# Encoder block on one core: block differences of the late phases on GpSimd, the output weights' differences made at the end of the attention's branch, an idle run of 11 products

## The chip, the cores and the metric

One core of a Trainium2 chip runs the whole kernel. The core has five engines that run side by side, each with its own queue of instructions: TensorE (PE, matrix products into PSUM), VectorE (DVE), ScalarE (ACT), GpSimd (POOL) and SyncE (SP, which issues most of the DMAs). SBUF is the on-chip memory that all of them read and write, DRAM the large memory behind the DMAs. The metric is the device time of one execution in microseconds (us); lower is better. A time is given as the median of several runs.

## The reference

One encoder block works on a stream of 16 learned tokens and 1024 positions, each of width 1024, in float32. Cut to what matters here:

```python
u = rms_norm(h, pre_w)
z = u @ w_in                            # 1024 x 7680; split into ten parts
rq, rk, rv, rg, aq, ak, av, ag, gr, ga = split(z)
o_r = group_norm(bidirectional_retention(rq, rk, rv)) * silu(rg)     # 4 heads
y_r = o_r @ w_rb
o_a = windowed_attention(aq, ak, av, sink) * silu(ag)                # 8 heads, 2 groups
y_a = o_a @ w_ab
mix = sigmoid(gr) * y_r + sigmoid(ga) * y_a
out = h + rms_norm(mix @ w_o, post_w)   # the 16 learned tokens are dropped
```

Four large products come last: the gate columns of `w_in` (rg, ag, gr, ga: 4096 columns), then `w_rb`, `w_ab` and `w_o` (1024 x 1024 each). They are the four late phases of the kernel.

## The kernel before, in words

**Arithmetic.** Every float32 operand of a product is split in a high part, rounded to TensorE's format (a cast, mostly on ACT), and a low part, operand minus high part (a subtraction, `dve_lo`, on DVE). `mm3` (lines 74 to 79) makes each product of three matmuls: high by high (L76), low by high (L77), high by low (L78). A matmul of the late phases has 128x128 weights and 512 columns.

**The stages in order.** The beginning loads the input, computes the norm and the first projections (0 to about 38 us). Before the first real product stands a run of idle products of zeros into a PSUM bank that nobody reads (`idle`, L310 to L313); their operand `xm` is ready very early, while the first real operand needs a load, a scaling and a split. Retention and attention follow, with their projections, until about 545 us. Then come the late phases.

**The late phases** are run by `class Phase` (L955 on): z (the 16 gate units of 256 columns, from about 545 to 797 us), r (`w_rb`, to 874), a (`w_ab`, to 951) and o (`w_out`, to 1036). A unit is a product of a 1024 x 256 left side with a 1024 x 1024 right side, each cut into 2 x 2 blocks, and is made with seven block products in place of eight (Winograd's form). A block product is a *job*: 4 x 3 matmuls. The right side of a phase (the transposed normed input in z, the gated branch output in r and a, `w_out` in o) has seven forms, each with high and low part: the blocks B11, B21, B22 and the differences T1 to T4, all held in SBUF for the whole phase. The left side's forms are made unit by unit: `prepare` (L979) makes a job's sums on DVE and then splits them (`split`, L973: cast on ACT, low part on DVE) into `lh` and `ll`. There are 6 buffers of each, and `run` (L1193) lets `prepare` go 6 jobs ahead of the job that it issues to PE (LEAD = 6). In the profile `lhz` and `llz` are the two parts in phase z; `llr`, `lla`, `llo` those of the other phases. The tile `bz`, `br`, `ba`, `bo` is the PSUM bank of a job.

**The hand-over from phase to phase.** Near the end of a phase, when a form of the old right side has been read for the last time, its place is filled with the same form of the next phase's. `refill(nm, src)` (L1143) gives a table from a job's number, counted back from the phase's end (-16 to -1), to what is done behind that job. Through z and r:

- loads of the four blocks of the new right side, each as four pieces 128x512 (256 KB) in buffers of `stage` (tags sg0 with 7 and sg1 with 8 buffers);
- `plain(...)`: `split_b` of a piece (L950; cast on ACT, low part on DVE) into its place among the forms;
- `minus(...)` (L1154, its instruction at L1155): one block difference of a piece, 128x512, on DVE. T1 = B12 - B11, T2 = B22 - B11, T3 = B22 - B12, T4 = B21 - B11, up to the names of the buffers, so 4 differences for each of the four T's, 16 at a hand-over. Each is written over one of its sources, and split after that.

At the third hand-over, a to o, the table is another one (`if nm == "a"`): only B11, B21 and B22 are loaded and split. The four differences of `w_out` were made long before, in phase z. There, behind the jobs 12k + 16 for k = 0 to 3, `pre_load` (L764) loads four pieces of `w_out`; behind the jobs 12k + 22 `pre_split` (L771) makes of them four differences on DVE (L776), four casts on ACT (L778), four low parts on DVE, and stores each of the eight results to DRAM (`pre_d`, L69). A list `near` holds the latest addition that a phase made out of PSUM on DVE, and a difference is ordered behind that one (`issue_after`). At the hand-over `get_pre` (L1128) loads the finished parts into their places, 8 loads of 1 MB or 768 KB and 2 of 256 KB.

**Other work in the late phases.** `combine` (L1052 on) adds the products of a unit out of PSUM on DVE and copies some on ACT; `z_post` scales and gates the results and stores them, `y_post` (L1275) multiplies by the gates, and in phase a adds to the stored sum `mx_d` by four accumulating DMAs that POOL issues (L1289); `o_post` makes the norm, the residual and the output.

**What sets the order.** Each engine takes its instructions strictly in the order of its queue; it waits, with all that is behind, where an operand is not there. The order within a queue is set when the kernel is built, by a planner that works from the order of the Python calls, its own cost model of the engines, and `issue_after`. DMAs of one queue are issued in the order of that queue too: nearly all loads and stores of the late phases are on SP's, those at L1289 on POOL's.

Of the kernel before, what the change touches and what calls it, by code (L numbers as in the profile page):

```python
# [7 lines left out]
F32 = mybir.dt.float32  # L8
R = mybir.dt.float32r
AF = mybir.ActivationFunctionType  # L10
ALU = mybir.AluOpType
# [5 lines left out]
P = 128  # L17
# [22 lines left out]
def block_kernel(ctx: ExitStack, tc: tile.TileContext, x0, xT, x, meta, w_in, w_rb, w_ab, w_out, post_w,  # L40
                 rope, tab, out):
    nc = tc.nc
# [12 lines left out]
    def bank(tag, name):  # L55
# [10 lines left out]

    e_d = {(u, p): dram.tile([P, 512], F32, tag=f"e{u}{p}", name=f"e{u}_{p}") for u in PRE for p in PRE[u]}
    xs_d = [dram.tile([4, P, 2, 512], F32, tag=f"xs{i}", name=f"xs{i}") for i in range(2)]
    pre_d = {n: [dram.tile([P, 4, 512], F32, tag=f"pre{n}{s}", name=f"pre{n}{s}") for s in range(2)]  # L69
             for n in ("T1", "T2", "T3", "T4")}  # L70

    latest = []

# [17 lines left out]
    def dve_lo(o, i, hi):  # L91
        return nc.vector.tensor_tensor(o, i, hi.bitcast(F32), ALU.subtract).ins  # L92
# [173 lines left out]
    with tc.tile_pool(name="setup", bufs=1, reuse_waits="tile") as st:  # L266
# [42 lines left out]

        idle = pj("idle")  # L310
        zeros = xm.rearrange("p k e -> p (k e)")
        for i in range(8):
            nc.tensor.matmul(idle[:, 0:KT * (32 + NM)], zeros[:, 0:P], zeros, start=True, stop=True)  # L313


# [12 lines left out]
        for k in range(KT):  # L328
            t = xr[k]
# [431 lines left out]

    xsum = {}

    def pre_load(k, src):  # L764

        w[k] = {}
        for i, j in ((0, 0), (0, 1), (1, 1), (1, 0)):
            w[k][i, j] = t = stage(f"w{i}{j}{k}", 1)
            src(t, 4 * i + k, j)

    def pre_split(k, behind):  # L771

        x = w.pop(k)
        for n, o, a, b in SUMS:
            with tc.issue_after(behind):
                nc.vector.tensor_tensor(x[o], x[a], x[b], ALU.subtract)  # L776
            h, l = (stage(f"w{n}{k}{e_}", s, R) for s, e_ in enumerate("hl"))
            nc.scalar.copy(h, x[o])  # L778
            nc.sync.dma_start(pre_d[n][0][:, k], h.bitcast(F32))
            dve_lo(l, x[o], h)  # L780
            nc.sync.dma_start(pre_d[n][1][:, k], l.bitcast(F32))

    w, near = {}, []
    gates = [U_G + u for u in range(4)] + [U_AG + u for u in range(4)] + [U_GR + u for u in range(8)]

    def pre_fetch(u):
# [149 lines left out]
    def right(n, s, k):  # L936
        if n == "T4" and k == 3:
            return margins[s], lambda t: t.rearrange("p (a c) -> p a c", a=KT)
        return B[n][s][:, k], lambda t: t
# [4 lines left out]
    def stage(name, j=0, dt=F32):  # L944
        return (yp if j else lp).tile([P, 512], dt, tag=f"sg{int(j)}", bufs=8 if j else 7, name=name)
# [179 lines left out]
            return l[:14] + o[:5] + l[14:15] + o[5:] + l[15:]  # L1125
        return [(u + e_, p) for u in range(0, n, 2) for p in (ORDER if u else first) for e_ in range(2)]

    def get_pre(n):  # L1128
        for s in range(2):
            m = B[n][s].shape[1]  # L1130
            nc.sync.dma_start(B[n][s].bitcast(F32), pre_d[n][s][:, 0:m])
            if m < 4:
                d, as_ = right(n, s, m)
                nc.sync.dma_start(d.bitcast(F32), as_(pre_d[n][s][:, m]))

    def get_sum(n):
        for k in range(4):
            t = stage(f"x{n}{k}", n in ("T2", "T3"))
# [4 lines left out]
    def refill(nm, src):  # L1143

        x = {}

        def load(i, j):
            def f():
                for k in range(4):
                    x[i, j, k] = t = stage(f"{nm}{i}{j}{k}", j)  # L1150
                    src(t, 4 * i + k, j)
            return f

        def minus(o, a, b):  # L1154
            nc.vector.tensor_tensor(x[*o], x[*a], x[*b], sub)  # L1155

        def plain(n, i, j):
            def f():
                for k in range(4):
                    split_b(n, k, x[i, j, k])  # L1160
            return f

        def t1():
            for k in range(4):
                minus((0, 0, k), (0, 1, k), (0, 0, k))
                split_b("T1", k, x[0, 0, k])

        def t2():
            for k in range(4):
                minus((0, 0, k), (1, 1, k), (0, 0, k))  # L1170
                split_b("T2", k, x[0, 0, k])

        def t3():
            for k in range(4):
                minus((0, 1, k), (1, 1, k), (0, 1, k))

        def b21():
            for k in range(4):
                split_b("B21", k, x[1, 0, k])
                minus((0, 0, k), (1, 0, k), (0, 0, k))  # L1180

        def got(n):
            return lambda: get_pre(n)

        if nm == "a":
            return {-16: [load(0, 0)], -14: [load(1, 1)], -13: [plain("B11", 0, 0)], -11: [got("T1")],
                    -10: [load(1, 0)], -9: [got("T2")], -7: [plain("B21", 1, 0)], -5: [got("T3")],
                    -3: [plain("B22", 1, 1)], -1: [got("T4")]}
        return {-16: [load(0, 0), load(0, 1)], -14: [load(1, 1)], -13: [plain("B11", 0, 0)], -11: [t1],
                -10: [load(1, 0)], -9: [t2, t3], -7: [b21], -5: [plain("T3", 0, 1)], -3: [plain("B22", 1, 1)],  # L1190
                -1: [plain("T4", 0, 0)]}

    def run(phases):  # L1193
# [7 lines left out]

        for u in (0, 1):
            hooks.setdefault(len(jobs) - len(ph_o.seq) - 11 + u, []).insert(0, lambda u=u: ph_o.block(u, "A11"))
        for k in range(4):
            hooks[12 * k + 16] = [lambda k=k: pre_load(k, act_src(w_out))]
            hooks[12 * k + 22] = [lambda k=k: pre_split(k, near[0])]
        n = 0
        for i, (ph, u, p) in enumerate(jobs):
            while n < min(i + LEAD, len(jobs)):
# [475 lines left out]
```

## Time and profile before

Three runs of the kernel took 1042.65, 1043.71 and 1046.04 us. The profiled execution took 1044.06 us; its trace spans 1042.3 us from the first to the last instruction.

| what | value |
|---|---|
| median of the runs | 1043.71 us |
| profiled execution | 1044.06 us |
| span of its trace | 1042.3 us |
| mean granted TensorE clock | 0.998 of full speed |
| instructions | 17315, of which 5880 matmuls |

The page of the profile has, in its second part, the span in 40 equal slices of 26 us, each digit the busy share of that slice in tenths:

```profile
## 2 busy tenths in 40 slices
PE   8999999999999999999999999999999999999997
PEld 8998999989989888988888888777888788788886
DVE  7786769758876778778769988998899899778665
ACT  5541332523423466664676554555557446334443
POOL 3345244243342433444310000000000000111032
PEclk9999999999999999999999999999999999999999
```

The late phases are the slices from the 21st on. In them DVE is at 8 or 9 tenths up to the 34th, the hand-over from r to a, and POOL does next to nothing from the 23rd to the 34th. Slices are means: a wait of one microsecond does not show in them.

A list of waits has a line for each engine and tile: who waited, for what, how many us in total, how often, and the longest. A table of stretches gives the busy time of each engine in one stretch of time. A timeline gives the start and the duration of every instruction. Busy times of PE are partly modelled, since matmuls overlap in its pipeline; the number of matmuls that start in a stretch is the safer reading.

### The profile page before, as it was taken

The page shows a single profiled execution, that of the slowest core. Times are in us where ns is not written, and L with a number is a line of the kernel's source. Part 1 is how long each engine was busy: PE and PEld are TensorE (multiplying, and loading weights), DVE is VectorE, ACT ScalarE, POOL GpSimd, SP SyncE. Part 2 cuts the span into 40 slices and gives each one's busy share as a digit, 9 for nine tenths or more (in the row PEclk, how much of TensorE's full clock was granted, in tenths as well). Part 3 has the DMA queues.
Part 4 walks back from the last instruction along what each step waited for, and adds up shares of the span by engine and source line. Part 5 has one row for each costly group of instructions (what it writes and reads, how often), then busy time and mean ns, then how long its engine had stood idle before and what let it go on. Part 6 is the DMA issues. An engine that isn't in the chain of part 4 may idle for free. (4 is left out here: it accounts for less than half of the span.)

```text
span 1042.3 us, 17315 instructions
## 1 busy us (share of the span) xinstructions
PE 1025.3 (98%) x5880; PEld 898.8 (86%) x5880; DVE 834.9 (80%) x1802; ACT 502.5 (48%) x1129; POOL 227.9 (22%) x368
## 2 busy tenths in 40 slices
PE   8999999999999999999999999999999999999997
PEld 8998999989989888988888888777888788788886
DVE  7786769758876778778769988998899899778665
ACT  5541332523423466664676554555557446334443
POOL 3345244243342433444310000000000000111032
PEclk9999999999999999999999999999999999999999
DMA  9434123243241467675558679899925746789464
GB/s 355 164 84 90 62 45 89 76 79 112 80 93 62 102 174 188 179 194 157 171 174 322 216 255 311 309 317 346 392 106 178 251 156 222 234 219 336 130 122 81
DMA packets 98841, 188.45 MB, mean 181 GB/s; under 512 B 13025, under 2 KB 37633, under 8 KB 98193
## 3 DMA queue, kind: packets, MB, share of 16 engines
q1 hardware_dynamic: 81200, 162.89, 46.4%
q0 software_dynamic: 10176, 14.73, 9.5%
q10 hardware_dynamic: 7376, 9.73, 2.7%
q8 instruction: 46, 0.75, 0.3%
q14 instruction: 43, 0.34, 0.1%
HBM read 124.32 MB, written 57.68 MB: 175 GB/s over the span
## 5 line engine op out<-in xcount | busy, mean ns | idle before, releaser
L1289 POOL DMA_DIRECT2D mx_d<-c1a x4 | 3.6, 890 | 398.1 <-DVE c1a L1280 398.1
L77 PE MATMUL bz<-big,llz 128*128 128x512 f32 x192 | 74.8, 390 | 0.3 <-DVE llz L92 0.3
L76 PE MATMUL bz<-big,lhz 128*128 128x512 f32 x192 | 74.0, 390 | 1.1 <-ACT lhz L976 1.1
L78 PE MATMUL bz<-big,lhz 128*128 128x512 f32 x192 | 74.2, 389 | 0.0
L76 PE MATMUL pv<-wh,big 128*128 128x256 f32 x256 | 72.8, 284 | 0.0
L77 PE MATMUL pv<-wh,big 128*128 128x256 f32 x256 | 72.7, 284 | 0.0
L78 PE MATMUL pv<-wl,big 128*128 128x256 f32 x256 | 72.7, 284 | 0.0
L76 PE MATMUL bz<-T,lhz 128*128 128x512 f32 x176 | 68.2, 390 | 1.4 <-DVE u2z L1066 1.3
L77 PE MATMUL bz<-T,llz 128*128 128x512 f32 x176 | 68.6, 390 | 0.9 <-DVE llz L92 0.9
L78 PE MATMUL bz<-T,lhz 128*128 128x512 f32 x176 | 68.5, 389 | 0.0
L76 PE MATMUL paq<-big,wh 128*128 128x512 f32 x128 | 51.5, 403 | 0.0
L1429 ACT ACTIVATE p<-raw,nm 128x337 f32<-128x337 f32 (+1 forms) x64 | 35.5, 556 | 33.1 <-DVE nm L1426 31.6
L77 PE MATMUL paq<-big,wl 128*128 128x512 f32 x128 | 50.3, 393 | 0.0
L78 PE MATMUL paq<-big,wh 128*128 128x512 f32 x128 | 50.2, 392 | 0.0
L1442 POOL TENSOR_SCALAR p<-p,den 128x336 f32<-128x336 f32 (+2 forms) x60 | 34.6, 624 | 66.7 <-DVE den L1433 64.1
L76 PEld LDWEIGHTS pv<-wh,big 128*128 128x128 f32 x256 | 48.4, 189 | 0.4
L77 PEld LDWEIGHTS pv<-wh,big 128*128 128x128 f32 x256 | 48.3, 189 | 0.4
L78 PEld LDWEIGHTS pv<-wl,big 128*128 128x128 f32 x256 | 48.2, 188 | 0.3
L76 PEld LDWEIGHTS bz<-big,lhz 128*128 128x128 f32 x192 | 36.0, 188 | 8.8 <-ACT lhz L976 1.5
L92 DVE TENSOR_TENSOR wl<-wr,wh 128x1024 fp32r<-128x1024 f32 x28 | 35.1, 1257 | 10.0 <-POOL wh L89 6.8
L77 PEld LDWEIGHTS bz<-big,llz 128*128 128x128 f32 x192 | 36.0, 188 | 8.1 <-DVE llz L92 0.6
L78 PEld LDWEIGHTS bz<-big,lhz 128*128 128x128 f32 x192 | 36.0, 188 | 7.5
(621 smaller groups left out, 3592.8 us busy)
## 6 DMA issues: line engine op xcount, KB each, us to landing
wrz<-in_w_in_dram SPq DMA_DIRECT2D x32, 512.0 KB, 6.1
wr<-in_w_in_dram SPq DMA_DIRECT2D x29, 512.0 KB, 4.1
we<-in_w_in_dram SPq DMA_DIRECT2D x16, 512.0 KB, 4.3
tg<-tg_d SPq DMA_DIRECT2D x32, 256.0 KB, 4.9
e<-e ACTq DMA_DIRECT2D x20, 256.0 KB, 2.6
e<-e SPq DMA_DIRECT2D x20, 256.0 KB, 4.7
xn<-in_x_dram SPq DMA_DIRECT2D x8, 512.0 KB, 9.0
oTr_d<-ost SPq DMA_DIRECT2D x16, 256.0 KB, 2.1
```

Of the source, the lines that this page charges most:

```text
L76: nc.tensor.matmul(o, ah, bh, start=first, stop=False, **kw)
L77: nc.tensor.matmul(o, al, bh, start=False, stop=False, **kw)
L78: latest[:] = [nc.tensor.matmul(o, ah, bl, start=False, stop=last, **kw).ins]
L92: return nc.vector.tensor_tensor(o, i, hi.bitcast(F32), ALU.subtract).ins
L1289: nc.gpsimd.dma_start(d, to, accum_op=ALU.add)
L1429: last["exp"] = nc.scalar.activation(pp[:, x_, w0 - o:w0 - o + 1 + wid], r[:, 0:1 + wid], AF.Exp, scale=-1.0, bias=nm_[:, x_:x_ + 1], accu ...
L1442: nc.gpsimd.tensor_scalar(v, v, den[:, x_:x_ + 1], 1.0, op0=ALU.mult, op1=ALU.mult)
```

## The change

- The idle run at the beginning has 11 products in place of 8.
- `minus` in `refill` is an instruction of GpSimd (`nc.gpsimd.tensor_tensor`) in place of VectorE.
- `pre_load`, `pre_split`, `get_pre`, the DRAM tiles `pre_d` and the two hooks in phase z that called them are gone. So is the table of its own for the hand-over from a to o: `w_out` is now loaded, subtracted and split at the end of phase a, by the same table as at the other two hand-overs.

```diff
@@ block_kernel @@
-    pre_d = {n: [dram.tile([P, 4, 512], F32, tag=f"pre{n}{s}", name=f"pre{n}{s}") for s in range(2)]
-             for n in ("T1", "T2", "T3", "T4")}
...
-        for i in range(8):
+        for i in range(11):
             nc.tensor.matmul(idle[:, 0:KT * (32 + NM)], zeros[:, 0:P], zeros, start=True, stop=True)
...
-    def pre_load(k, src):
-
-        w[k] = {}
-        for i, j in ((0, 0), (0, 1), (1, 1), (1, 0)):
-            w[k][i, j] = t = stage(f"w{i}{j}{k}", 1)
-            src(t, 4 * i + k, j)
-
-    def pre_split(k, behind):
-
-        x = w.pop(k)
-        for n, o, a, b in SUMS:
-            with tc.issue_after(behind):
-                nc.vector.tensor_tensor(x[o], x[a], x[b], ALU.subtract)
-            h, l = (stage(f"w{n}{k}{e_}", s, R) for s, e_ in enumerate("hl"))
-            nc.scalar.copy(h, x[o])
-            nc.sync.dma_start(pre_d[n][0][:, k], h.bitcast(F32))
-            dve_lo(l, x[o], h)
-            nc.sync.dma_start(pre_d[n][1][:, k], l.bitcast(F32))
-
-    w, near = {}, []
+    near = []
@@ get_pre @@
-    def get_pre(n):
-        for s in range(2):
-            m = B[n][s].shape[1]
-            nc.sync.dma_start(B[n][s].bitcast(F32), pre_d[n][s][:, 0:m])
-            if m < 4:
-                d, as_ = right(n, s, m)
-                nc.sync.dma_start(d.bitcast(F32), as_(pre_d[n][s][:, m]))
-
@@ refill @@
         def minus(o, a, b):
-            nc.vector.tensor_tensor(x[*o], x[*a], x[*b], sub)
+            nc.gpsimd.tensor_tensor(x[*o], x[*a], x[*b], sub)
...
-        def got(n):
-            return lambda: get_pre(n)
-
-        if nm == "a":
-            return {-16: [load(0, 0)], -14: [load(1, 1)], -13: [plain("B11", 0, 0)], -11: [got("T1")],
-                    -10: [load(1, 0)], -9: [got("T2")], -7: [plain("B21", 1, 0)], -5: [got("T3")],
-                    -3: [plain("B22", 1, 1)], -1: [got("T4")]}
         return {-16: [load(0, 0), load(0, 1)], -14: [load(1, 1)], -13: [plain("B11", 0, 0)], -11: [t1],
                 -10: [load(1, 0)], -9: [t2, t3], -7: [b21], -5: [plain("T3", 0, 1)], -3: [plain("B22", 1, 1)],
                 -1: [plain("T4", 0, 0)]}
@@ run @@
-        for k in range(4):
-            hooks[12 * k + 16] = [lambda k=k: pre_load(k, act_src(w_out))]
-            hooks[12 * k + 22] = [lambda k=k: pre_split(k, near[0])]
```

Counted over the whole kernel, DVE has 48 instructions fewer (32 from the gates, 32 differences of the two hand-overs, and 16 low parts more at the third), POOL 48 more, ACT as many as before (16 casts moved from the gates to the third hand-over), SP 54 DMAs fewer (16 loads, 32 stores and 10 loads gone, 4 loads new) and PE three matmuls more.

## The prediction

> **What bounds the kernel now.** I read the page's busy times, then TensorE's list of waits, then busy times in stretches of 20 us, then the timelines.
>
> ```profile
> span 1042.3 us, 17315 instructions
> PE 1025.3 (98%) x5880; PEld 898.8 (86%) x5880; DVE 834.9 (80%) x1802; ACT 502.5 (48%) x1129; POOL 227.9 (22%) x368
> ```
>
> PE (TensorE) is busy 98% of the span, so only the 17.0 us in which it is not, or in which it runs slowly, can be won. The list of waits (engine, line, for whom, us in total, times) has the phases z (gates), r and a (branches):
>
> ```profile
> PE bz L76 <- DVE u2z L1066: 1.3, 1, 1.3
> PE bz L77 <- DVE llz L92: 1.2, 2, 0.9
> PE bz L76 <- ACT lhz L976: 1.1, 1, 1.1
> PE ba L77 <- DVE lla L92: 0.9, 1, 0.9
> PE br L77 <- DVE llr L92: 0.8, 2, 0.6
> ```
>
> Each waits for VectorE (DVE) or for ScalarE's cast beside it. The stretches say where:
>
> ```profile
> 640.00:660.00 20.00, 20.00 (x89) 16.55 (x89) 16.79 (x28) 9.22 (x16) 0.00 (x0) 1.00 0.89 312
> 660.00:680.00 20.00, 18.80 (x82) 15.00 (x81) 18.07 (x31) 8.32 (x15) 0.00 (x0) 1.00 0.97 342
> 680.00:700.00 20.00, 18.69 (x83) 15.18 (x82) 20.00 (x34) 11.93 (x21) 0.00 (x0) 1.00 0.94 296
> 700.00:720.00 20.00, 20.00 (x90) 16.55 (x89) 16.79 (x29) 10.04 (x18) 0.00 (x0) 1.00 1.01 366
> 720.00:740.00 20.00, 19.06 (x85) 15.45 (x84) 17.68 (x30) 10.55 (x19) 0.00 (x0) 1.00 0.98 357
> ...
> 780.00:800.00 20.00, 20.00 (x90) 16.55 (x89) 20.00 (x34) 15.31 (x28) 0.00 (x0) 1.00 0.44 144
> 800.00:820.00 20.00, 19.20 (x84) 15.23 (x83) 19.62 (x33) 10.48 (x19) 0.00 (x0) 1.00 0.85 284
> ...
> 860.00:880.00 20.00, 20.00 (x90) 16.57 (x89) 20.00 (x34) 13.53 (x25) 0.00 (x0) 1.00 0.59 206
> 880.00:900.00 20.00, 19.11 (x83) 15.14 (x82) 19.19 (x32) 9.06 (x16) 0.00 (x0) 1.00 0.82 279
> 900.00:920.00 20.00, 20.00 (x90) 16.58 (x89) 15.29 (x26) 6.09 (x11) 5.24 (x6) 1.00 0.75 184
> 920.00:940.00 20.00, 20.00 (x90) 16.57 (x89) 12.32 (x19) 8.27 (x15) 1.74 (x3) 1.00 0.88 248
> 940.00:960.00 20.00, 20.00 (x90) 16.54 (x89) 17.69 (x31) 9.42 (x16) 1.75 (x2) 1.00 0.96 336
> ```
>
> The columns are PE, weight loads, DVE, ACT and POOL (GpSimd), each in us with its instructions in brackets, then clock, DMA share and GB/s. A full stretch starts 90 products, 0.222 us each. Missing products are lost time: 8 + 7 + 5 = 20 in the gates (4.4 us), 6 where z hands over to r (1.3 us), 7 where r hands over to a (1.6 us). In these stretches DVE is near or at 20 of 20, while POOL has nothing to do from 640 to 900. The hand-over from a to o loses nothing: DVE is idle there for 4.71 + 7.68 + 2.31 = 14.7 us.
>
> The beginning (start, duration, what):
>
> ```profile
> 1.36 2.93 PE L313 MATMUL idle<-xm 128*128 128x384 f32 x8 [1.36 <-DVE warm L207]
> 5.53 0.77 PE L76 MATMUL pq<-big,w 128*128 128x512 f32 x1 [1.24 <-ACT big L333]
> ...
> 7.41 0.63 PE L76 MATMUL pq<-big,w 128*128 128x512 f32 x1
> 7.83 0.63 PE L77 MATMUL pq<-big,w 128*128 128x512 f32 x1
> ...
> 10.65 0.39 PE L76 MATMUL pq<-big,w 128*128 128x512 f32 x1
> 10.88 0.39 PE L77 MATMUL pq<-big,w 128*128 128x512 f32 x1
> ```
>
> A 512-column product starts 0.42 us after the one before until about 10.6 us, and 0.23 us after it from then on: half pace for the first 5.1 us of real work (5.53 to 10.65), after an idle run of 2.93 us and a gap of 1.24 us. The clock column of the stretches does not show this.
>
> **The change, part by part.** Durations are from this one execution, 1044.06 us (span 1042.3), which lies 0.35 us above the median 1043.71 of the runs; I subtract from the execution and then take off 0.35.
>
> ```profile
> L776 DVE TENSOR_TENSOR w<-w,w x16: 679/681/685, 616.8 to 721.0; 128x512 f32<-128x512 f32 x16
> L313 PE MATMUL idle<-xm x8: 522/522/687, 1.4 to 3.8; 128*128 128x384 f32 x8
> L1155 DVE TENSOR_TENSOR z<-z,z 128x512 f32<-128x512 f32 x16 | 10.7, 682 | 0.0
> L195 POOL TENSOR_TENSOR qr<-m_qk,m_qk 128x512 f32<-128x512 f32 x2 | 2.6, 1288 | 4.1 <-DVE m_qk L194 2.7 <-DVE ms L378 1.4
> 780.35 1.89 DVE L1155 TENSOR_TENSOR z<-z,z 128x512 f32<-128x512 f32 x3
> 688.12 0.68 DVE L92 TENSOR_TENSOR wT12l<-w,wT12h 128x512 fp32r<-128x512 f32 x1
> ```
>
> Three in a row take 1.89, so one costs DVE (1.89 - 0.68) / 2 = 0.60 us.
>
> 1. Out of the gates: 16 differences (L776) and 16 low parts (the wT row's kind), 32 x 0.60 = 19.2 us of DVE from 616.8 us to shortly after 721.0 (first and last start of L776); 16 casts on ACT; 16 loads and 32 stores of 256 KB on SP's queue. The lost 20 products lie in that stretch, behind a DVE without a gap. Taking out 4.8 us for each of the four parts leaves DVE some 15 of 20, as in the full stretches. Gain between 0 (if it was the DMA that held the operands) and 4.4; I take 4.4, because the list names DVE and ACT and no DMA.
>
> 2. Idle run 8 to 11: three more at (2.93 - 0.69) / 7 = 0.32 us (0.687, the longest of the eight, for the first to pass through) end at 4.29 + 0.96 = 5.25, before the operand of 5.53. They delay nothing. If full pace follows 5.1 us after an unbroken run begins, as in the rows, and the run now begins at 1.36, it comes at 6.5: slow work falls from 5.1 to 1.0 us, worth (5.1 - 1.0) / 2 = 2.1 us. If the remaining gap of 0.28 still breaks the run, nothing. I take 1.6, nearer to the upper end, since the gap shrinks to a quarter. The order in which PE takes the first pieces changes a little too; no wait stands there, so 0.
>
> 3. Differences of z to r and r to a, 16 each, from DVE to POOL. DVE is freed 16 x 0.60 = 9.6 us at each hand-over; POOL works 16 x 1.29 = 20.6 us in stretches of some 45 us, so it is not the bound by itself. But the engines get in each other's way when both read SBUF:
>
> ```profile
> 54.37 0.41 DVE L92 TENSOR_TENSOR Slf<-Sf,Shf 128x256 fp32r<-128x256 f32 x1
> 57.60 1.26 DVE L92 TENSOR_TENSOR Slf<-Sf,Shf 128x256 fp32r<-128x256 f32 x1
> 57.48 2.29 POOL L89 TENSOR_SCALAR wh<-wr 128x1024 fp32r<-128x1024 f32 x2
> 492.77 0.98 DVE L802 TENSOR_TENSOR we<-we,we 128x512 f32<-128x512 f32 x1
> 492.73 2.19 POOL L1442 TENSOR_SCALAR p<-p,den 128x272 f32<-128x272 f32 x2
> ```
>
> Beside POOL instructions of 2.29 / 2 = 1.15 us, Slf took 1.26 instead of 0.41: 0.85 lost, 0.74 of POOL's time. Beside one of 1.10, the 512-wide operation took 0.98 instead of 0.68: 0.30 lost, 0.27. For a difference of 1.29 us that is 0.35 to 0.95 us of DVE. Where DVE reads PSUM or has nothing to do it loses nothing, which pulls the lower end to 0. I take 0.60, between the two rows: DVE loses what it was freed of, and both hand-overs keep their waits (0 us).
>
> The order also matters. Each cast and low part of a difference now stands in ACT's and DVE's queues behind POOL's result, and the operands of PE (lhr, llr, lha, lla) stand behind those. POOL can keep up: a region of B comes free with every second or fourth product pair, 5.4 us, in which POOL makes four.
>
> 4. a to o: 16 differences on POOL instead of 10 loads (8.4 MB), 16 casts more on ACT and 16 low parts more on DVE, 4 loads of 256 KB more. DVE gets 9.6 us of low parts and 16 x 0.60 = 9.6 lost to POOL, 19.2 us. The cover is the idle 14.7 and what the first operand that follows has in hand:
>
> ```profile
> 964.20 0.69 DVE L92 TENSOR_TENSOR llo<-sto0S,lho 128x512 fp32r<-128x512 f32 x1
> 969.95 0.39 PE L77 MATMUL bo<-big,llo 128*128 128x512 f32 x1
> 942.37 0.88 POOL L1289 DMA_DIRECT2D mx_d<-c1a  x1 [18.55 <-DVE c1a L1280]
> ```
>
> It is ready at 964.9 and used at 969.95, 5.1 us later. 14.7 + 5.1 = 19.8 against 19.2: just covered; I take 1.0 us of loss for idle time that comes too early, with 0 and 8 as ends (8 at 0.95 lost per difference and 2 us of idle out of reach). POOL issues four accumulating DMAs in this stretch; the first now stands behind 14 differences, up to 18 us of work that starts near 926, and may go out some 5 us late. c1a's buffers are next written 20 us after that row: 0.
>
> Sum: -4.4 - 1.6 + 0 + 0 + 1.0 = -5.0, 1039.1 on the execution, 1038.7 by the median.
>
> **The rivals.** SBUF port, the slower side: all hangs on what a POOL difference takes from DVE. PE already waits at both hand-overs, and a to o has 0.6 us left, so each 0.1 us beyond 0.60 costs up to 48 x 0.1 = 4.8 us. At 0.70 the whole gain is gone. At 0.85 (the Slf row's 0.95 with one DVE operation in eight reading PSUM, as the order of instructions has it) it is +12.0: 1050.7. For it: DVE reads two SBUF operands nearly everywhere there. Against it: the 0.30 of the other row.
> The Trainium skill, "SBUF — State Buffer", section "Who interferes with whom", says that a DVE instruction with two SBUF inputs and a GpSimd instruction that reads SBUF exclude each other, and that the second to start is blocked until the first has finished. By that rule the lost time would be 1.29 each, 48 x 0.69 = 33 us more than I take, 1072 with no cover at all, as an estimate; the row at 57.60 agrees with it, the one at 492.77 only in part.
>
> POOL hidden: at 0.35 lost, DVE gains 4 us at each hand-over, the 1.3 and 1.6 us of waits go and a to o costs nothing: -4.4 - 1.6 - 2.9 = -8.9, 1034.8. For it: POOL's idle stretch is long.
>
> It does little: the clock rises no earlier and a to o loses 3.5 us: -0.9, 1042.8. For it: an idle run of 2.93 us brought no early clock, and the last low parts of B come in a crowd.
>
> **How the numbers follow.** Forecast (1036.5 to 1040.5) 0.36, hidden (below 1036.5) 0.14, little 0.22, port 0.28. No change means within 0.3%, 1040.6 to 1046.8, about what a measurement can tell. So faster 0.50, same 0.22, slower 0.28. The range reaches from the hidden case to the port's, 1034.5 to 1050.5; the forecast's own is 1036.5 to 1040.5.
>
> **What would show it.** Step 1: 89 or 90 products in every 20 us from 660 to 740. Step 2: 0.23 us between products from about 7 us on. Step 3: L1155 on POOL near 1.3 us, low parts on DVE near 0.68; the port case shows them well above 0.68 and PE waiting longer for llr and lla. Step 4: PE waiting for llo near 970 us tells what a to o costs. The prediction is wrong if PE's waits at the three hand-overs grow by more than 5 us together.

## The result and the profile after

The changed kernel takes 1072.67 us (median of 5 runs, 1069.98 to 1075.69), the kernel before 1043.46 us (5 runs): ratio 1.0278, 95% interval 1.0254 to 1.0302. It is 29 us slower, where I had forecast 5 us faster, and lies 22 us above the top of my range. The profiled execution took 1069.98 us. Line numbers are shifted by 2 to 39: L74 to L76 are the three matmuls, L90 the low parts, L931 the casts of the right side, L1042 the copies out of PSUM, L1126 the differences.

The page's busy times, and PE's list of waits (for whom, us in total, times, longest):

```profile
PE 1032.2 (97%) x5883; PEld 903.8 (85%) x5883; DVE 853.7 (80%) x1754; ACT 501.3 (47%) x1129; POOL 306.6 (29%) x416
```
```profile
PE ba L74 <- ACT u3a L1042: 12.0, 1, 12.0
PE bz L74 <- ACT u3z L1042: 6.5, 1, 6.5
PE br L75 <- DVE llr L90: 2.6, 1, 2.6
PE br L74 <- DVE u3r L1045: 2.5, 1, 2.5
```

DVE has 48 instructions fewer and is busy 18.8 us longer. The four long waits lie at the three hand-overs and add up to 23.6 us; a growth there of more than 5 us was my sign of being wrong. The stretches of 20 us (columns as in the prediction):

```profile
660.00:680.00 20.00, 19.51 (x86) 15.86 (x85) 15.39 (x26) 8.19 (x15) 0.00 (x0) 1.00 0.72 254
680.00:700.00 20.00, 19.16 (x85) 15.53 (x85) 14.91 (x25) 8.04 (x14) 0.00 (x0) 1.00 0.89 302
...
780.00:800.00 20.00, 13.54 (x53) 10.78 (x52) 20.00 (x21) 8.77 (x17) 11.86 (x8) 0.83 0.29 97
...
860.00:880.00 20.00, 17.25 (x71) 13.63 (x70) 20.00 (x17) 9.78 (x18) 16.31 (x11) 0.94 0.17 44
880.00:900.00 20.00, 17.51 (x68) 13.89 (x67) 20.00 (x33) 10.80 (x20) 1.97 (x2) 0.89 0.93 299
...
940.00:960.00 20.00, 19.41 (x86) 15.75 (x84) 19.97 (x14) 10.65 (x19) 18.04 (x12) 1.00 0.17 53
960.00:980.00 20.00, 8.61 (x27) 6.91 (x28) 18.48 (x28) 5.47 (x11) 7.36 (x6) 0.66 0.38 90
```

Of the 90 products that a full stretch starts, 37 are missing at z to r, 19 + 22 = 41 at r to a, 4 + 63 = 67 at a to o: 8.2, 9.1 and 14.9 us at 0.222 each, 32.2 together, against 13 products (2.9 us) before. In the gates 4 + 5 = 9 are missing in place of 20, a gain of 2.4 us. The hand-overs lose 32.2 - 2.9 = 29.3 us more than before; less the 2.4 of the gates that is 26.9, and the spans differ by 25.9 (1068.2 against 1042.3). So the whole loss is at the hand-overs.

Look at DVE's columns: from 860 to 880 it is busy for all of 20 us and finishes 17 instructions, 34 in the same stretch before. The timeline shows what they do. POOL's differences (the row of the line: shortest, median, longest ns; first and last start), then DVE's at two places and POOL's beside them (start, duration, what):

```profile
L1126 POOL TENSOR_TENSOR z<-z,z x16: 1265/1736/1746, 765.0 to 798.7; 128x512 f32<-128x512 f32 x16
```
```profile
769.46 3.48 DVE L90 TENSOR_TENSOR llz<-wrz,lhz 128x512 fp32r<-128x512 f32 x2
772.86 1.77 DVE L90 TENSOR_TENSOR llz<-stz14S,lhz 128x512 fp32r<-128x512 f32 x1
774.56 1.78 DVE L90 TENSOR_TENSOR big<-z,big 128x512 fp32r<-128x512 f32 x1
```
```profile
875.15 0.68 DVE L1045 TENSOR_TENSOR c1r<-c1r,br 128x512 f32<-128x512 f32 x1
```
```profile
767.31 18.68 POOL L1126 TENSOR_TENSOR z<-z,z 128x512 f32<-128x512 f32 x11 [0.63 <-DVE big L90]
875.30 1.27 POOL L1126 TENSOR_TENSOR r<-r,r 128x512 f32<-128x512 f32 x1 [0.63 <-DVE T L90]
```

From 769.46 to 774.56 DVE starts one instruction every 1.70 us (three intervals in 5.10) in place of every 0.60, and POOL one difference every 18.68 / 11 = 1.70. This reads as if the engines took turns, 0.60 for DVE and 1.70 - 0.60 = 1.10 for POOL. A POOL difference then costs DVE 1.10 us, more than the 0.60 that it costs when DVE does it. The last row of each engine shows the exception: `c1r<-c1r,br` has one operand in PSUM, and takes its usual 0.68 while POOL's difference runs, which then takes 1.27. The median of 1736 ns says that most of the 16 differences had to take turns.

So DVE falls behind by up to 16 x (1.10 - 0.60) = 8.0 us at each hand-over, against the same differences on DVE. How this reaches PE is seen best at a to o (four engines' timelines, in this order: DVE, SP's queue, ACT, PE):

```profile
963.83 0.68 DVE L1241 SCALAR_TENSOR_TENSOR c1a<-tg,c1a 128x512 f32<-128x512 f32 x1
```
```profile
964.53 0.33 SPq L1228 DMA_DIRECT2D tg<-tg_d  x1
965.17 0.34 SPq L1186 DMA_DIRECT2D a<-in_w_out_dram  x1
```
```profile
970.23 0.62 ACT L931 CAST big<-a 128x512 fp32r<-128x512 f32 x1 [11.18 <-DMA a<-in_w_out_dram]
970.75 0.58 ACT L1042 COPY u3a<-ba 128x512 f32<-128x512 f32 x1
```
```profile
971.39 0.80 PE L74 MATMUL ba<-T,lha 128*128 128x512 f32 x1 [11.98 <-ACT u3a L1042]
971.98 0.63 PE L75 MATMUL ba<-T,lla 128*128 128x512 f32 x1
972.41 0.63 PE L76 MATMUL ba<-T,lha 128*128 128x512 f32 x1
```

DVE's late `c1a` sets a gate buffer free; only then does SP issue the load of gates that waited for it, and behind it the load of the eighth piece of `w_out`; ACT stands 11.18 us before the cast of that piece, with the copy of `u3a` out of PSUM behind it in its queue; PE waits 11.98 us for that bank. And when it goes on, it starts a product every 0.43 us, half pace, although the list of waits shows nothing any more.

At the beginning the idle run closed the gap, and full pace came earlier:

```profile
1.36 3.89 PE L311 MATMUL idle<-xm 128*128 128x384 f32 x11 [1.36 <-DVE warm L205]
5.41 0.76 PE L74 MATMUL pq<-big,w 128*128 128x512 f32 x1 [0.15 <-ACT big L331]
```
```profile
7.27 0.43 PE L74 MATMUL pq<-big,w 128*128 128x512 f32 x1
7.54 0.40 PE L75 MATMUL pq<-big,w 128*128 128x512 f32 x1
```

The gap is 0.15 us. The products at 7.27 and 7.54 already stand 0.27 us apart, those from 9.18 to 9.41 us 0.23; before the change the pace was half until 10.6 us.

### The profile page after: what moved, and what is told of

Same layout as the page of the kernel before. It is cut to its first block, busy times and chain, and to the rows that moved or that the text cites. A ratio compares the mean times of both kernels' runs of the same rounds, so it can differ in the third digit from the quotient of the medians.

```text
span 1068.2 us, 17277 instructions
## 1 busy us (share of the span) xinstructions
PE 1032.2 (97%) x5883; PEld 903.8 (85%) x5883; DVE 853.7 (80%) x1754; ACT 501.3 (47%) x1129; POOL 306.6 (29%) x416
## 5 line engine op out<-in xcount | busy, mean ns | idle before, releaser
L1126 POOL TENSOR_TENSOR z<-z,z 128x512 f32<-128x512 f32 x16 | 26.3, 1668 | 244.7 <-DVE big L90 236.6
L74 PE MATMUL bz<-T,lhz 128*128 128x512 f32 x176 | 69.0, 394 | 6.5 <-ACT u3z L1042 6.5
L76 PE MATMUL bz<-big,lhz 128*128 128x512 f32 x192 | 74.1, 389 | 0.0
L74 PE MATMUL bz<-big,lhz 128*128 128x512 f32 x192 | 74.1, 389 | 0.0
L74 PE MATMUL pv<-wh,big 128*128 128x256 f32 x256 | 72.8, 284 | 0.0
L76 PE MATMUL pv<-wl,big 128*128 128x256 f32 x256 | 72.7, 284 | 0.0
L76 PE MATMUL bz<-T,lhz 128*128 128x512 f32 x176 | 68.9, 392 | 0.0
L74 PE MATMUL paq<-big,wh 128*128 128x512 f32 x128 | 51.6, 403 | 0.0
L76 PE MATMUL paq<-big,wh 128*128 128x512 f32 x128 | 50.2, 392 | 0.0
L74 PEld LDWEIGHTS pv<-wh,big 128*128 128x128 f32 x256 | 48.4, 189 | 0.4
L76 PEld LDWEIGHTS pv<-wl,big 128*128 128x128 f32 x256 | 48.2, 188 | 0.3
L185 POOL DMA_DIRECT2D aq<-m_aq x32 | 27.5, 979 | 62.2 <-DVE aq L183 34.3
L74 PEld LDWEIGHTS bz<-T,lhz 128*128 128x128 f32 x176 | 33.4, 190 | 13.8 <-ACT u3z L1042 6.9
L90 DVE TENSOR_TENSOR wl<-wr,wh 128x1024 fp32r<-128x1024 f32 x28 | 35.2, 1259 | 10.4 <-POOL wh L87 6.7
```

The source lines that it names most:

```text
L74: nc.tensor.matmul(o, ah, bh, start=first, stop=False, **kw)
L76: latest[:] = [nc.tensor.matmul(o, ah, bl, start=False, stop=last, **kw).ins]
L185: nc.gpsimd.dma_start(o[64 - r:128 - r, 0:n], m[r:r + 64, 0:n], accum_op=ALU.add)
L1126: nc.gpsimd.tensor_tensor(x[*o], x[*a], x[*b], sub)
```

## The experiments

All times are medians, the ratios are to the kernel before on the same chip, whose median was 1041.66 to 1043.38 us. The theory: a GpSimd subtraction takes 1.10 us from DVE, and DVE's lateness passes on to PE. Rivals: PE waits for GpSimd's late results and for what stands behind them; or the new table at a to o does the harm whatever engine subtracts. A second question is what held back the gates before.

### The idle run alone

```diff
-        for i in range(8):
+        for i in range(11):
```

> The kernel before with the idle run of 11 products alone. In the trace of the changed kernel the 512-column products are at full pace from 7.3 us instead of 10.6, the 50th real product starts 1.46 us earlier (14.34 against 15.80), but phase z begins only 0.54 us earlier. Theory (the clock rises earlier, and the attention gives part of it back): 0.5 to 1.5 us faster, 1042.0 to 1043.0. Rival (the earlier pace is all lost again in the attention, whose order is fixed by other engines): within 0.3 us, 1043.2 to 1043.8.

1041.70 us, ratio 0.9995 (0.9985 to 1.0005): 0.5 us by the ratio, with no gain at all inside the interval. What is won at the beginning is mostly lost again before the gates: in this trace phase z begins at 546.6 us, 0.7 us earlier than before.

### GpSimd at two hand-overs, the rest as before

```diff
-            nc.vector.tensor_tensor(x[*o], x[*a], x[*b], sub)
+            nc.gpsimd.tensor_tensor(x[*o], x[*a], x[*b], sub)
```

> The kernel before with the differences of z to r and r to a on GpSimd; w_out's stay in the gates, the idle run stays at 8. Theory of the port (each GpSimd difference holds DVE's two-operand instructions for 1.1 us, and this alone makes the loss): the same loss as in the changed kernel at these two hand-overs, 6.9 + 7.8 us by the count of products, so about 1058. Rival (the loss at r to a was made by the changed table of the third hand-over, whose loads and orders begin there): 6.9 us and no more than 1 us beside it, 1050 to 1051.

1057.19 us, ratio 1.0143 (1.0124 to 1.0162), about 15 us lost, for 32 differences. 32 x 0.50 = 16. The waits at z to r and r to a are those of the changed kernel (6.5, 2.6 and 2.5 us), so they are the differences' own and not the work of the third hand-over.

### The changed kernel with all differences on DVE

```diff
-            nc.gpsimd.tensor_tensor(x[*o], x[*a], x[*b], sub)
+            nc.vector.tensor_tensor(x[*o], x[*a], x[*b], sub)
```

> The changed kernel with all 48 differences back on DVE. Theory of the port: the gains at the beginning and in the gates stay (0.5 and 2.9 us by the count of products), z to r and r to a lose 1.3 and 1.6 us as before, and a to o loses 0 to 2 us, since 19.2 us of added DVE work stand against 19.8 us of cover: 1039.5 to 1042.5. Rival (the new table at a to o loses time whatever engine subtracts, by the late load of the eighth piece and the casts and copies that stand behind it on ACT): a wait of 5 us or more near 960 us, 1045 to 1052.

1046.47 us, ratio 1.0038 (1.0025 to 1.0051). The engine of the differences is worth 1.0278 - 1.0038 = 0.024, 25 us; 48 x 0.50 = 24. But it is not the gain that I expected. The waits at z to r and r to a are as small as before; a to o loses. Its stretches there, and PE's rows:

```profile
920.00:940.00 20.00, 20.00 (x90) 16.54 (x89) 19.97 (x34) 13.56 (x25) 0.00 (x0) 1.00 0.32 88
940.00:960.00 20.00, 19.97 (x88) 16.25 (x87) 20.00 (x35) 11.53 (x20) 1.75 (x2) 1.00 0.37 92
960.00:980.00 20.00, 17.39 (x63) 13.55 (x63) 15.63 (x28) 5.47 (x10) 1.72 (x2) 0.83 0.42 106
```
```profile
968.03 1.45 PE L74 MATMUL bo<-big,lho 128*128 128x512 f32 x2 [2.61 <-ACT lho L955]
```

DVE is full from 920 on, but 3.94 us of 900 to 920 stay idle (it is busy for 16.06 of 20): the table of the hand-over lets its arithmetic begin behind the 13th job before the phase's end, near 920. The cover that could be reached was 7.68 + 2.31 + 5.1 = 15.1 us, against 19.2. PE waits 2.61 us, and then runs at half pace for 6 us more: 2 + 27 products are missing, 6.4 us.

### The load of the eighth piece from ACT's queue

```diff
-                    src(t, 4 * i + k, j)
+                    src(t, 4 * i + k, j, nc.scalar if (i, j, k) == (1, 0, 3) else nc.sync)
```

> The changed kernel, with the load of the eighth piece of each hand-over issued from ACT's queue in place of SP's, where it stood behind a load of gates that waited 15.8 us for DVE. The order of DVE and GpSimd is the same. Theory A (the 12 us wait at a to o ends with that load's landing, and the load could go 5 us earlier): PE's wait of 12.0 us shrinks to 6 to 8, the time to 1064 to 1069. Theory B (DVE's backlog behind the port sets the end, the load is only the last link): less than 1.5 us, 1071 to 1074.

1070.06 us, ratio 1.0263 (1.0247 to 1.0279); the interval overlaps that of the changed kernel. PE's wait is 12.7 us in place of 12.0. Issued from ACT, the load still went out no earlier than 966.53, just behind a low part of DVE (965.78 + 0.68 us):

```profile
965.78 0.68 DVE L90 TENSOR_TENSOR big<-a,big 128x512 fp32r<-128x512 f32 x1
```
```profile
966.53 0.34 ACTq L1186 DMA_DIRECT2D a<-in_w_out_dram  x1
```

So the load was the last link of the chain, and DVE's lateness stood before it.

### A GpSimd subtraction that nobody waits for

```diff
             nc.vector.tensor_tensor(x[*o], x[*a], x[*b], sub)
+            nc.gpsimd.tensor_tensor(junk, x[*o], x[*o], sub)
```

> The changed kernel with the differences on DVE, and behind each of the 48 a GpSimd subtraction of the same size whose result (bf16, in a tile of its own) nobody reads. It adds no work to DVE and no operand that PE or ACT waits for. Theory of the port (a GpSimd subtraction takes 1.1 us of DVE's time where DVE's instructions have two SBUF operands, and DVE's lateness passes on to PE one for one): 48 x 1.1 = 53 us more than without them (1046.5), if all meet busy DVE; 1080 to 1100. Rival (the loss comes of waiting for GpSimd's late results, and of what stands behind them on ACT): nobody waits for these, 1045 to 1049.

1082.12 us, ratio 1.0389 (1.0366 to 1.0412): 36 us more than without the extra subtractions, although in the trace no engine and no DMA waits for them. PE's longest waits are now for DVE's low parts (`llr`, `lla`, `llz`). DVE's timeline beside them:

```profile
788.54 1.53 DVE L90 TENSOR_TENSOR llz<-wrz,lhz 128x512 fp32r<-128x512 f32 x1
789.99 1.52 DVE L90 TENSOR_TENSOR big<-z,big 128x512 fp32r<-128x512 f32 x1
```

One every 1.45 us: this form (bf16 result) takes 0.85 from DVE, 48 x 0.85 = 41 us if all meet it. The rival of late results falls: the loss comes without anyone waiting for GpSimd. Whether it is GpSimd's reading or its writing, two further kernels below tell.

### Four of sixteen on GpSimd

```diff
-                minus((0, 0, k), (0, 1, k), (0, 0, k))
+                minus((0, 0, k), (0, 1, k), (0, 0, k), nc.gpsimd)
```

> The changed kernel with 4 of the 16 differences of each hand-over (T1's) on GpSimd, the other 12 on DVE. Theory of the port, with each difference on GpSimd costing DVE 1.1 us in place of 0.6: 12 x 0.5 = 6 us more than all on DVE (1046.5), 1051 to 1054. Rival (a few differences hide in GpSimd's idle stretch, and only a chain of 12 in a row does harm): 1045 to 1048.

1052.21 us, ratio 1.0088 (1.0065 to 1.0111), 0.0050 or 5.2 us above all on DVE; 12 x 0.50 = 6. The price of one difference is about the same for 12, 32 and 48 of them (5.2, 15 and 25 us, so 0.43, 0.47 and 0.52 us each; the 5.2 is known to some 2.7 us either way): between 12 and 48 no threshold shows, and little or nothing of the price is hidden.

### A copy, and a fill, in place of the extra subtraction

```diff
-            nc.gpsimd.tensor_tensor(junk, x[*o], x[*o], sub)
+            nc.gpsimd.tensor_copy(junk, x[*o])       # the second kernel: two fills, memset(junk, 0.0)
```

> As the kernel with the 48 extra GpSimd subtractions, but each is a copy with a single input (same tile read, same bf16 result that nobody reads). If any GpSimd instruction that reads SBUF holds DVE's two-operand instructions until it ends, DVE's low parts take 1.2 us or more beside a copy, and the time is 1065 to 1090. If it takes two GpSimd inputs to fill the port, DVE stays near 0.68 us and the time near 1046.

> The same with 96 fills of that tile on GpSimd, which read nothing (they wait for nothing, so they run where GpSimd first is free of other work, beside the busy DVE of the gates). If the reading of SBUF is what excludes, DVE's instructions beside them stay near 0.68 us and the time within 1044 to 1049; if any GpSimd instruction does it, they lengthen by the fill's duration.

One run each: 1063.42 us with the copies, 1043.07 with the fills (before, on that chip, 1043.38). The rows of the copies and of DVE beside them, and then the same of the fills:

```profile
L1127 POOL CAST junk<-z x16: 927/952/5157, 767.7 to 801.2; 128x512 bf16<-128x512 f32 x16
```
```profile
791.44 1.09 DVE L1203 TENSOR_TENSOR c1z<-c1z,rbc 128x512 f32<-128x512 f32 x1
792.46 1.09 DVE L90 TENSOR_TENSOR llz<-wrz,lhz 128x512 fp32r<-128x512 f32 x1
```
```profile
L1127 POOL MEMSET junk<- x48: 524/524/526, 545.8 to 600.5; 128x512 bf16 x48
```
```profile
565.09 1.89 DVE L90 TENSOR_TENSOR T<-xT,T 128x512 fp32r<-128x512 f32 x3
```

Beside copies DVE starts an instruction every 1.02 us (0.42 lost), beside fills every 0.60 (nothing lost). A single input is enough; these fills, which only write, take nothing. 48 x 0.42 = 20 us. The time with the copies lies just under my 1065 to 1090, since a copy takes less from DVE than the 0.5 or more that I had: less than half of the 0.93 us that a copy lasts where it is shortest. The time with the fills lies just under my 1044 to 1049.

### The gates: arithmetic left out, stores left out

```diff
-                nc.vector.tensor_tensor(x[o], x[a], x[b], ALU.subtract)
...
-            nc.sync.dma_start(pre_d[n][0][:, k], h.bitcast(F32))
+                nc.sync.dma_start(pre_d[n][s][:, k], x[o])    # s = 0, 1; no cast, no low part
```

> The kernel before whose gates keep the 16 loads and 32 stores of w_out's preparation but leave out its arithmetic: the loaded pieces are stored as they are in place of the differences' parts, so the last product is computed from other operands. Theory 1 (DVE's 19.2 us hold back the gates, as the prediction had it): the 2.9 us gained there by the change come with this one too, 1039.5 to 1041. Theory 2 (the DMAs hold the gates back: their share is 0.94 to 1.01 from 660 to 740 us before, 0.60 to 0.89 after the change): nothing gained, 1042 to 1043.5.

```diff
-            nc.sync.dma_start(pre_d[n][0][:, k], h.bitcast(F32))
+            if not k:
+                nc.sync.dma_start(pre_d[n][0], h.bitcast(F32))     # the low parts alike
```

> The kernel before, whose gates keep all of w_out's arithmetic (16 differences, 16 casts, 16 low parts) and loads, but store the parts of the first pieces alone (8 stores in place of 32; at the end of a the first pieces are loaded in place of all, so the last product is computed from other operands). Theory 1 (DVE's 19.2 us hold back the gates): nothing gained, 1042 to 1043.5. Theory 2 (the DMAs hold them back): 2 to 3 us gained from 660 to 740 us, 1039.5 to 1041.

Without the arithmetic 1045.01 us, ratio 1.0025 (1.0013 to 1.0037); without 24 of the stores 1041.34, ratio 0.9993 (0.9984 to 1.0001). Their stretches in the gates, first two without arithmetic, then two without stores:

```profile
600.00:620.00 20.00, 17.96 (x71) 14.06 (x70) 12.80 (x21) 7.42 (x15) 0.00 (x0) 0.91 1.03 380
```
```profile
640.00:660.00 20.00, 18.76 (x83) 15.21 (x82) 15.50 (x27) 8.72 (x15) 0.00 (x0) 1.00 0.96 346
```
```profile
660.00:680.00 20.00, 19.47 (x86) 15.83 (x85) 18.73 (x32) 9.50 (x17) 0.00 (x0) 1.00 0.79 289
680.00:700.00 20.00, 19.30 (x85) 15.42 (x84) 20.00 (x35) 11.21 (x19) 0.00 (x0) 1.00 0.88 266
```

Without DVE's 19.2 us a loss is there all the same (19 + 7 products), at a DMA share of 0.96 to 1.05, and DVE is idle beside it; it comes earlier, since the stores go out as soon as the pieces are loaded. With DVE's work but without most stores 9 products are missing from 660 to 740 us, as in the changed kernel, and DVE is as full as before. That speaks for the DMAs and against DVE's arithmetic, but it does not prove it. Each count is that of one trace. Three kernels whose gates do all of the old work lose 20, 21 and 13 products there (the one before, the idle run alone, GpSimd at two hand-overs), eight kernels whose gates do none of it 5 to 13. Nor is a full DMA share enough: from 620 to 640 us the kernel without arithmetic is at 1.04 and loses nothing. In time the second kernel gained nothing clear of noise, where 2 to 3 us were expected: in its trace phase z began 1.0 us later than before, and I cannot say why.

### w_out's differences made elsewhere, or issued elsewhere

All five of these kernels have the idle run of 11. In the first the gates make the 16 differences and store them unsplit (16 stores), and the end of a loads and splits them:

```diff
-            nc.scalar.copy(h, x[o]) ... dve_lo(l, x[o], h)
+            nc.sync.dma_start(pre_d[n][:, k], x[o])
...
+            -12: [fetch("T2", 0)], -11: [got("T1")], ...     # load the differences, split_b them
```

> A version that may beat both: the kernel before, idle run of 11; the gates make w_out's 16 differences on DVE and store them unsplit (16 stores in place of 32, no casts and low parts there), and the end of phase a loads them and splits them (16 casts on ACT, 16 low parts on DVE, 9.6 us, against 14.7 us in which DVE is idle there). If the cover holds: half of the gates' DVE work and of its stores gone, 1.5 to 3 us there and 0.3 at the beginning, 1039 to 1041. If the low parts come in a crowd at the end of a: a wait of 2 to 6 us for llo or lho near 960 us, 1043 to 1048.

1047.76 us, ratio 1.0055 (1.0038 to 1.0072). The end of a loses nothing any more: 9.6 us of low parts are covered. The gates lose more than before, where SP stands 6 us before a load whose buffer waits for a store to land (656.7 to 662.7 us; PE then waits 3.1 us for `u2z` and 2.9 for `lhz`). The time lies in the range that I gave for low parts in a crowd at the end of a, but that is not what happened.

The second makes the differences in the early r and a:

> A version that may beat both: as the last one (idle run of 11, w_out's 16 differences stored unsplit, split at the end of a), but the differences are made in the early r and early a phases (behind the 8th, 11th, 36th and 38th job from r's start) in place of the gates. There DVE has 5 us idle of 20 (820 to 840 us) and 4.7 and 7.7 (900 to 940), against 4.8 us for each pair of parts, and the DMAs have room. The gates then have no work for w_out, as in the changed kernel. Theory: 2.9 us gained in the gates, 0.3 at the beginning, nothing lost after: 0.3% faster than before, 1039 to 1041. Rival (the loads and stores stand in SP's queue among r's and a's own, and hold back gates or weights there): a new wait of 2 us or more in r or a, 1042.5 to 1046.

1051.07 us, ratio 1.0085 (1.0066 to 1.0104). The rival came: even in the profiled execution, the fastest at 1046.56, PE waits 3.2 us for `u3a` and 2.7 for `lla`. The median lies 5 us above that rival's range, and no trace shows what the other executions lost.

The third leaves the work of before and lets GpSimd issue w_out's loads and stores (`nc.gpsimd.dma_start`), the fourth does so with half the stores, as in the first:

> The kernel before with the idle run of 11, and w_out's 16 loads and 32 stores in the gates issued by GpSimd, which has nothing else to do there, in place of SP's queue. DVE's and ACT's work and the bytes moved are those of before. Theory Q (the gates lose their time because SP's queue waits for w_out's operands and buffers, and the unit weights and sums stand behind): 2 to 3 us gained from 660 to 740 us, 1038.5 to 1040.5. Theory B (the DMA engines are full there, share 0.94 to 1.01, whoever issues): no gain beside the idle run's, 1041 to 1043.

> The version that stores w_out's differences unsplit and splits them at the end of a (idle run of 11), with its 16 loads and 16 stores in the gates issued by GpSimd in place of SP's queue. In its first form the end of a lost nothing (4.75 us behind before it, 4.71 after), and the gates lost 6 us by SP's waiting 6 us for a buffer whose store had not landed. Theory Q: the gates now keep their pace, 2 to 3 us gained, 1038.5 to 1040.5. Theory B, with half the stores: 1 to 1.5 us, 1040 to 1041.5. Rival: the issue on GpSimd gets in DVE's way as its subtractions do, 1043 or more.

1044.45 us, ratio 1.0021 (1.0011 to 1.0030), and 1041.18, ratio 0.9991 (0.9979 to 1.0002). With all the stores another queue gains nothing, and its trace loses 24 products from 660 to 740 us. With half the stores the kernel is 0.9 us faster than before, about as theory B said, with an interval that just reaches no change. Against the first of these five kernels, which moves the same bytes, the other queue is worth 6.6 us (1.0055 - 0.9991): it takes away SP's wait of 6 us with all that stood behind it. So the queue matters where a transfer in it has to wait for a buffer. The last kernel moves the fourth's parts to an earlier time:

```diff
-            hooks[12 * k + 16] = [lambda k=k: pre_load(k, act_src(w_out))]
-            hooks[12 * k + 22] = [lambda k=k: pre_split(k, near[0])]
+            hooks.setdefault(6 * k + 16, []).append(lambda k=k: pre_load(k, act_src(w_out)))
+            hooks.setdefault(6 * k + 22, []).append(lambda k=k: pre_split(k, near[0]))
```

> The version with half the stores, issued by GpSimd, with w_out's four parts behind the jobs 16 to 40 of the gates (6 apart) in place of 16 to 58 (12 apart), so mostly before 660 us, where the DMA share is 0.63 to 0.9. Theory B (the DMAs are full from 660 to 740 us): the 15 products that were missing there come back to the 9 of the changed kernel, 1 to 1.5 us, 1039 to 1040.5. Against it: DVE is at 19.7 of 20 from 560 to 600, and the loss only moves there, 1041 to 1043.

1039.16 us (1038.13 to 1039.86), ratio 0.9962 (0.9948 to 0.9976): it beats both kernels, the one before by 4 us. Its gates:

```profile
660.00:680.00 20.00, 19.47 (x86) 15.82 (x85) 18.32 (x31) 8.22 (x14) 1.75 (x4) 1.00 1.02 348
680.00:700.00 20.00, 20.00 (x90) 16.54 (x89) 19.76 (x33) 10.59 (x19) 0.00 (x0) 1.00 0.97 344
```

4 products are missing in place of 20. From 640 to 660 and from 680 to 700 the DMA share is 0.99 and 0.97, and nothing is lost there.

## Why the prediction was wrong

**What bounds the kernel** was read rightly in one half. The missing products were counted and placed rightly. But I took the DVE column, near 20, for the cause of the gates' loss. The DMA share of 0.94 to 1.01 stood in the same rows, two columns further, and is the likelier cause: leaving out the arithmetic kept a loss, leaving out the stores brought it down to that of the changed kernel. The spread between traces leaves it short of shown.

**Part 1 (gates, -4.4).** The gain came, 11 products or 2.4 us in place of 20 or 4.4, and probably by another way: the stores and loads went with the arithmetic. My argument "the list names DVE and ACT and no DMA" was too short. The list names the last link alone. Before PE's wait for DVE at 699.08, DVE had itself stood 1.77 us for a load of weights, and was full from there on:

```profile
677.85 0.69 DVE L1002 TENSOR_TENSOR stz8S<-wrz,wrz 128x512 f32<-128x512 f32 x1 [1.77 <-DMA wrz<-in_w_in_dram]
```

For PE's wait at 669.85 no such load is found; there DVE was full without a break.

**Part 2 (idle run, -1.6).** The mechanism was right: the gap shrank to 0.15 us and full pace came earlier. The error was to carry a gain at 10 us to the end of the kernel. By itself the step is worth 0.5 us with 0 inside its interval.

**Part 3 (differences to GpSimd, 0).** This step failed, and with it the sum. I took 0.60 us of DVE per difference, between 0.35 and 0.95; it is 1.10, outside my own bounds. The bounds came from single overlaps of one POOL instruction with one of DVE, each taken as a share of POOL's length. But what such a row holds is how long one DVE instruction was blocked, and that depends on when it came within POOL's. A chain of twelve against a DVE with a full queue has no such luck: each DVE instruction meets the start of the next difference, and pays all of it but the last 0.17 (1.27 - 1.10). The lower bound rests on a misreading besides. I took the 1.10 us of POOL's instruction beside the DVE row of 492.77 for its own length. Undisturbed, two of the same form take 0.97 us, 0.49 each:

```profile
497.48 0.97 POOL L1442 TENSOR_SCALAR p<-p,den 128x272 f32<-128x272 f32 x2 [1.78 <-DVE den L1433]
```

So POOL was held up in that overlap too. DVE came 0.04 us behind the start of a POOL instruction of 0.49; with 0.17 at the end free, full exclusion would cost it 0.49 - 0.04 - 0.17 = 0.28 us, as an estimate, and it lost 0.30. The row that I held against the port fits it.

With 1.10 in the place of 0.60, 48 x 0.50 = 24 us are added to the sum, 1039.1 + 24 = 1063. The other three parts make up most of the rest: 2.0 us that the gates gained less than forecast, 1.1 of the idle run, and 6.4 - 1.0 = 5.4 at a to o, which gives 1071.6 against 1072.67. The rival of the port named the mechanism, the place and the break-even (0.70) rightly; its price of 0.85 was too low too.

The Trainium skill, "SBUF — State Buffer", section "Who interferes with whom", says that a DVE instruction with two SBUF inputs and a GpSimd instruction that reads SBUF exclude each other for the whole instruction, and that neither a DVE instruction with at most one SBUF input (outside the modes in which DVE uses both its ports for one input) nor a GpSimd instruction that only writes is concerned. Who is concerned agrees with the runs: 1.10 us lost beside differences, 0.42 beside copies, none beside fills, none for the addition out of PSUM. "The whole instruction" agrees only roughly for a difference (1.10 of 1.27 us) and not for a copy (0.42 of 0.93). By that rule my estimate gave 1072, the measured time, and I weighed it down by the row of 492.77. That the number was met is in part luck: the estimate charged 1.29 us for each difference, 33 us more than my sum, where 1.10 each make 24, and the errors of the other parts filled the rest.

**Part 4 (a to o, +1.0).** Wrong by its own share: on DVE alone the new hand-over loses 6.4 us, inside the 0 to 8 that I gave (the 8 was reckoned with the contention, so this is no hit), because 4.7 us of the idle time that I counted as cover lies before the work can start. With GpSimd it loses 14.9. That POOL's accumulating DMAs would cost nothing was right: the two with `c1a` went out at 964.88 and 971.55, at most 1.8 us behind DVE's results.

**What no part had:** the price of a wait does not end with it. After the wait of 2.61 us PE ran at half pace for 6.4 us, after those of 6.5 and 12.0 for 3.2 and 5.3. At z to r 6.5 us of waiting became 8.2 us of missing products, at r to a 5.1 became 9.1. My prices counted the waits alone.

## What to carry to other kernels

Before moving work from VectorE to GpSimd, ask whether both will read SBUF at the same time: where VectorE is full of instructions with two SBUF inputs, count nearly the whole length of a GpSimd subtraction as lost to VectorE, which here was more than doing it there (1.10 us against 0.60). Price a contention by a stretch in which both queues are full and not by single overlaps, and set the length that an instruction has undisturbed beside the length that it has in the overlap. Read the DMA share in the same row before blaming the engine that is busy, and count several traces before trusting a difference of ten products. Idle time covers new work only from the moment when that work's inputs and places are there.

## What was not expected of the hardware

- DVE and GpSimd take turns one for one once both wait: 1.70 us per pair with 128x512 float32 subtractions on both. But GpSimd can also be starved. In the kernel with extra subtractions the first of a chain took 5.57 us, in that with copies up to 5.16, while DVE issued two-operand instructions every 0.60 us; it came to its turn when DVE had an instruction with an operand in PSUM (785.65 and 785.01 us). Which of the two happens is not settled here.
- A wait of PE of 1.31 us (before 699.08 in the kernel before) brought no half pace. Waits of 2.02 us (before 614.68, gates without arithmetic) and of 2.61 us did. Half pace ended 3.4 us after the first and 6.4 us after the second (968.03 to 974.4); elsewhere 3.2 (after the wait at 789) to 5.3 us after the wait. The Trainium skill, "TensorE: Matmul & The Clock Gate", section "Part 1: The HAM clock gate", has the slow clock come after an idle window of about 3.4 us, and the full clock after a busy one, with windows whose start is not tied to the work. One to two such busy windows would be 3.4 to 6.8 us, as an estimate from the page's figure, and the 3.2 to 6.4 us lie near that; the drop came here after 2.02 and 2.61 us of waiting (2.4 and 3.0 us between two starts), shorter than the page's window.
- The DMA share of a stretch reached 1.0 with 340 to 390 GB/s. Some such stretches lost products (0.97 from 660 to 680 us before, 8 products) and others none (1.01 from 700 to 720 us before): the share alone does not tell.
